# Two transformer blocks on one core: attention products in split passes, gates behind both halves, a shorter second norm

## The chip, the core and the metric

The kernel runs on one core of one Trainium2 chip. TensorE multiplies matrices, VectorE and ScalarE do elementwise work, GpSimd does a little of it and issues some transfers, and SP issues most transfers. The metric is the device time of one execution in microseconds (us).

## What is computed

The reference applies a first block (a gated mix of a convolution, a linear recurrence and stick-breaking attention, and a feed-forward part) and then a second block of two layers. The change touches the two layers, and one norm of the first block. A layer of the second block, with 512 positions, model width 1024 and 8 heads of width 128:

```python
x = x + 0.5 * swiglu(rms_norm_2(x, ffn1_norm[l]), ...)
h = rms_norm_2(x, mix_norm[l])
proj = h @ w_in[l] + b_in[l]
q, k, v, f_logit, xr, gr, g_attn, g_rnn = jnp.split(proj, SPLIT_POINTS, axis=-1)
q, k = rms_norm_2(q per head, q_norm[l]), rms_norm_2(k per head, k_norm[l])
log_f = jax.nn.log_sigmoid(f_logit)
y_attn = forgetting_attention(q, k, v, log_f) @ w_o_attn[l]
xr = causal_depthwise_conv(xr, conv_w[l], conv_b[l])
yr = rg_lru(xr, ...) * jax.nn.gelu(gr)
y_rnn = yr @ w_o_rnn[l]
merged = sigmoid(g_attn) * y_attn + sigmoid(g_rnn) * y_rnn
x = x + merged @ w_out[l]
x = x + 0.5 * swiglu(rms_norm_2(x, ffn2_norm[l]), ...)
```

`forgetting_attention` adds to the scaled scores of a causal softmax the difference of the running sums of `log_f` at the query and at the key. `rg_lru` is a gated linear recurrence over the positions.

## The kernel before

Activations lie transposed, as eight tiles of 128 channels by 512 positions, and every tile of 512 columns takes 2 KB of a partition.

**Split products.** A float32 matrix is kept as a high part rounded to float32r and the rest as a low part (`split`, line 221; `w`, line 182, does it for the weights). `mm3` (line 227) forms a product in three float32r passes: high by high, high by low, low by high. The projections are made in this way. Other products are plain float32 matmuls, which the profile lists as two records each: the scores (line 840), the values (line 865) and the recurrence's gates (lines 907 and 908). Transposes (lines 395 and 861) are matmuls against an identity, one record each.

**Weights** come in one order, written out in `_plan_layer`, through a ring of four chunks (`raw`, `hi`, `lo`): SP issues the load, ScalarE rounds (line 197), VectorE subtracts (line 198).

**Memory.** Tiles come from pools by tag, each tag with a number of buffers (`pool`, line 138). Pools are a stack: one that is opened after another was closed lies on the closed one's bytes. TensorE's results go to eight banks: four accumulators (`acc`, tag a), and four for everything else (xm, xh, two of xs). `tokens` (line 256) takes all four accumulators for a projection of queries, keys or values: for each weight chunk it runs the four token blocks in turn. `pair` (line 242) takes two.

**Order.** The framework orders each engine's instructions ahead of the run from a simulated timeline, by program order and with what stands under `hp()` first; a tile waits until a buffer of its tag is free.

**A mixing layer** (`mix`, line 959): the pool mb with 38 tiles (line 964). The recurrence's pool rn, 18 tiles and with them the tag xr, lives from line 983 to 1005: four pairs of projections, emptied by `scaled` (line 978) and line 1002 into xr, then `rnn` (line 892), which for each of eight tiles makes a convolution (lines 903 and 905), two products (907, 908), activations (910 to 914) and two multiplications (915, 916), and after every four tiles a square root (921), a product (923) and a scan (924). Then the forget gate: one accumulator `fa`, emptied into `fz` (line 1014), a scan, a transfer to memory (1021) from which `cb` is broadcast (884), and `ct` (1025). Then two halves of four heads each: queries, keys and values by `tokens`, emptied at line 1037, queries and keys normalised and transposed by `heads_T` into qkT (line 397), and `attn` (868). `attn_scores` (834) makes one block of 128 queries: product, bias (843), causal fill on GpSimd (845), maximum (848), exponential (849), scaling (851). `attn_values` (854) transposes the weights and multiplies them with the values, one block behind the scores; line 879 copies a finished head. After each half come the gates of the recurrence for that half (lines 1047 to 1059), written into tiles Y of a pool that is opened after the first half's attention (1045). Then the projections of the two branches with their gates, and the output projection.

**The second norm of the first block** (lines 578 to 594): line 583 adds the squares of each new tile to a running sum (`add_square`, line 305, whose addition is line 310); `stats` (296) then takes column products with ones (272), adds epsilon (280), takes the power on GpSimd (281), spreads the row by transposes (289) and copies it out (293), and lines 590 to 593 form the input of the feed-forward part.

Of the kernel before, what the change touches and what calls it, by code (L numbers as in the profile page):

```python
# [20 lines left out]
MIX = 3080  # L21
# [55 lines left out]
def _plan_layer(l):  # L77
# [4 lines left out]
    for hf in range(2):  # L82
        for o in (0, 1024, 2048):
            p += _rows("w_in_2", l, 8, o + hf * 512)
        for m in range(4 * hf, 4 * hf + 4, 2):
            p += _cols("w_in_2", l, 8, MIX + 1024 + m * 128)
# [32 lines left out]
class Build:  # L119
# [155 lines left out]

    def rsqrt(self, src, w, g="m"):
# [101 lines left out]
    def heads_T_(self, src, nh, dh, gain):  # L378
# [13 lines left out]
        for j in range(4):  # L392
# [3 lines left out]
            o = self.t("qkT")  # L396
            nc.scalar.activation(o, ps, AF.Copy, scale=gain)
            out.append(o)
# [164 lines left out]
    def first_block(self):  # L563
        nc = self.nc
        src = lambda i: self.ap["xT"][i * 128:i * 128 + 128, :]
        with ExitStack() as ctx:
# [5 lines left out]
            with ExitStack() as c1:  # L572
# [5 lines left out]
                for m in range(0, 8, 2):  # L578
                    for i, a in enumerate(self.pair("w_out", 0, 8, m * 128, mh)):
                        with self.hp():  # L580
                            nc.vector.scalar_tensor_tensor(x[m + i], a, self.mod[:, 16 + m + i:17 + m + i], x[m + i],
                                                           op0=OP.mult, op1=OP.add)
                            self.add_square(x[m + i], m + i == 0)
            self.pool(ctx, "mlp", act=32, t=4, mr=2)
            with self.hp():
                _, rb = self.stats()
# [247 lines left out]
    def attn_scores(self, qT, kT, i, hd, ct, cb):  # L834
# [5 lines left out]
        nc.tensor.matmul(ps[:, :n], qT[:, ts], kT[:, :n], start=True, stop=True)  # L840
# [13 lines left out]
    def attn_values(self, st, v, vc, i, o):  # L854

        nc = self.nc
        n = (i + 1) * 128
        pt = self.aux("xs")
        for j in range(i + 1):
            js = slice(j * 128, j * 128 + 128)  # L860
            nc.tensor.transpose(pt[:, js], st[:, js], self.ident)  # L861
        pT = self.t("pT")
        nc.scalar.copy(pT[:, :n], pt[:, :n])
        for j in range(i + 1):
            nc.tensor.matmul(o[:, i * 128:n], v[j][:, vc:vc + 128], pT[:, j * 128:j * 128 + 128],  # L865
                             start=(i == 0 and j == 0), stop=(i == 3 and j == 3), skip_group_check=True)

    def attn(self, qT, kT, v, hd0, ct, cdram):
# [3 lines left out]

        def values(st, hd, i):
            if i == 0:
                out.append(self.aux("xh"))
            self.attn_values(st, v, (hd - hd0) * 128, i, out[-1])
            if i == 3:
                y = self.t("x")
                nc.scalar.copy(y, out[-1])
                out[-1] = y  # L880

        for hd in range(hd0, hd0 + 4):
            cb = self.t("cb")
            nc.gpsimd.dma_start(cb, cdram[hd:hd + 1, :].to_broadcast([128, 512]))
            for i in range(4):
                todo.append((self.attn_scores(qT[hd - hd0], kT[hd - hd0], i, hd, ct, cb), hd, i))
                if len(todo) > 1:
                    values(*todo.pop(0))
        values(*todo.pop(0))
# [292 lines left out]
```

## Time and profile before

| | |
|---|---|
| median of 3 runs | 3414.53 us (3413.23 to 3414.99) |
| the profiled execution | 3413.82 us, its span 3412.0 us |
| TensorE busy | 3389.3 us, 15362 records |
| VectorE busy | 1879.7 us |
| ScalarE busy | 1308.1 us |
| GpSimd busy | 164.6 us |
| transfers | 351.30 MB, mean 103 GB/s |

The profile is one execution on the chip. Its page gives busy times of each engine, the span in 40 slices, and the chain of work that ended last; the trace answers for single lines, tiles and stretches. A matmul's record is longer than its slot, since matmuls overlap: the slot shows in the distance of starts, or in the chain, where each piece lasts until the next one begins.

### The profile page before, as it was taken

Reading aid. Unit: us, or ns where it says so; the run is one execution under the profiler, and the core shown is the slowest. Engines: PE = TensorE matmul, PEld = TensorE weight load, DVE = VectorE, ACT = ScalarE, POOL = GpSimd, SP = SyncE. Lnnn points to the kernel's source line nnn. Section 1 sums busy time; section 2 is a strip of 40 time slices with the busy share of each in tenths; the row PEclk is TensorE's granted clock in tenths of the full one; section 3 lists DMA queues with packets and bytes.
Section 4 is the critical chain, followed back from the end, with each engine's and each line's share of the span. In section 5 each row is a group of like instructions: output and inputs, shape, how many; then the busy total and the mean of one; then the engine's idle time right before and its main releaser. Section 6 shows DMA issues by size and latency. Waiting matters only on the chain.

```text
span 3412.0 us, 42001 instructions
## 1 busy us (share of the span) xinstructions
PE 3389.3 (99%) x15362; PEld 2767.3 (81%) x15362; DVE 1879.7 (55%) x3168; ACT 1308.1 (38%) x2283; POOL 164.6 (5%) x273
## 2 busy tenths in 40 slices
PE   8999999999999999999999999999999999999999
PEld 6887777888888888788888888888887788888887
DVE  7698654534444444876455444444447865454442
ACT  3335443423333333654333333333336544343331
POOL 0011000000000001111000000000010110000000
PEclk9999999999999999999999999999999999999999
DMA  6223433433333333323333333333333222333332
GB/s 217 72 78 106 154 112 107 130 98 97 96 96 97 96 117 105 90 91 89 111 97 95 99 97 97 95 99 96 103 123 95 86 89 81 123 95 98 96 105 91
DMA packets 179599, 351.30 MB, mean 103 GB/s; under 512 B 20672, under 2 KB 21952, under 8 KB 178368
## 3 DMA queue, kind: packets, MB, share of 16 engines
q1 hardware_dynamic: 173088, 329.05, 31.5%
q0 software_dynamic: 6160, 19.37, 1.9%
q8 instruction: 121, 1.98, 0.2%
q14 instruction: 86, 0.70, 0.1%
q10 hardware_dynamic: 144, 0.20, 0.0%
HBM read 342.21 MB, written 6.32 MB: 102 GB/s over the span
## 4 chain that ended last, share of the span: by engine, by line
PE 96%; DVE 2%; ACT 1%; issue 1%; DMA 0%; POOL 0%; SPq 0%; DVEq 0%; ACTq 0%
PE a L231 30%; PE a L229 30%; PE a L230 30%; PE xh L865 1%; PE xs L840 1%; PE xh L432 1%; PE xh L514 1%; PE xs L492 1%; PE xs L861 1%; PE xm L395 0%; DVE xc L905 0%; DVE mq L333 0%; DVE lo L198 0%; PE xh L508 0%; PE xh L471 0%
## 5 line engine op out<-in xcount | busy, mean ns | idle before, releaser
L198 DVE TENSOR_TENSOR lo<-raw,hi 128x512 fp32r<-128x512 f32 x1144 | 785.1, 688 | 1254.2 <-ACT hi L197 1239.7
L197 ACT CAST hi<-raw 128x512 fp32r<-128x512 f32 x1144 | 706.9, 619 | 1571.7 <-PE a L230 1270.4
L230 PE MATMUL a<-h,hi 128*128 128x512 f32 x2528 | 989.4, 392 | 0.0
L229 PE MATMUL a<-h,hi 128*128 128x512 f32 x2528 | 984.4, 392 | 2.3 <-ACT h L592 2.3
L231 PE MATMUL a<-h,lo 128*128 128x512 f32 x2528 | 982.3, 392 | 0.0
L229 PEld LDWEIGHTS a<-h,hi 128*128 128x128 f32 x2528 | 475.2, 188 | 106.4 <-issue 6.1
L231 PEld LDWEIGHTS a<-h,lo 128*128 128x128 f32 x2528 | 474.9, 188 | 105.2 <-issue 7.2
L230 PEld LDWEIGHTS a<-h,hi 128*128 128x128 f32 x2528 | 474.9, 188 | 101.4 <-issue 3.6
L229 PE MATMUL a<-act,hi 128*128 128x512 f32 x960 | 373.4, 389 | 0.0
L230 PE MATMUL a<-act,hi 128*128 128x512 f32 x960 | 373.4, 389 | 0.0
L231 PE MATMUL a<-act,lo 128*128 128x512 f32 x960 | 372.8, 389 | 0.0
L230 PE MATMUL a<-Y,hi 128*128 128x512 f32 x544 | 214.5, 394 | 0.0
L229 PE MATMUL a<-Y,hi 128*128 128x512 f32 x544 | 213.7, 393 | 0.0
L231 PE MATMUL a<-Y,lo 128*128 128x512 f32 x544 | 212.8, 391 | 0.0
L229 PEld LDWEIGHTS a<-act,hi 128*128 128x128 f32 x960 | 180.2, 188 | 37.5
L231 PEld LDWEIGHTS a<-act,lo 128*128 128x128 f32 x960 | 180.2, 188 | 37.5
L230 PEld LDWEIGHTS a<-act,hi 128*128 128x128 f32 x960 | 180.2, 188 | 37.3
L231 PE MATMUL a<-hi,h 128*128 128x512 f32 x512 | 204.5, 403 | 0.0
L230 PE MATMUL a<-lo,h 128*128 128x512 f32 x512 | 203.7, 398 | 0.0
L229 PE MATMUL a<-hi,h 128*128 128x512 f32 x512 | 199.2, 407 | 1.7 <-DVE qk L1037 1.7
L231 PEld LDWEIGHTS a<-Y,lo 128*128 128x128 f32 x544 | 102.2, 188 | 23.4 <-issue 2.1
L230 PEld LDWEIGHTS a<-Y,hi 128*128 128x128 f32 x544 | 102.2, 188 | 23.1 <-issue 2.0
(293 smaller groups left out, 3049.3 us busy)
## 6 DMA issues: line engine op xcount, KB each, us to landing
raw<-in_w_l SPq DMA_DIRECT2D x852, 256.0 KB, 2.6
raw<-in_w_first SPq DMA_DIRECT2D x284, 256.0 KB, 2.6
mr<-in_mod_b_ SPq DMA_DIRECT2D x32, 512.0 KB, 3.8
mq<-in_mod_a SPq DMA_DIRECT2D x8, 1024.0 KB, 8.1
xs<-x POOLq DMA_DIRECT2D x16, 256.0 KB, 2.4
cb<-cd POOLq DMA_DIRECT2D x16, 256.0 KB, 3.5
x<-xs POOLq DMA_DIRECT2D x16, 256.0 KB, 3.9
bq<-in_brow POOLq DMA_DIRECT2D x12, 256.0 KB, 3.8
```

The lines of the kernel that those rows point to most:

```text
L197: nc.scalar.copy(hi, raw)
L198: nc.vector.tensor_tensor(lo, raw, hi.bitcast(F32), op=OP.subtract)
L229: mm(acc, w[0], x[0], start=start, stop=False)
L230: mm(acc, w[0], x[1], start=False, stop=False)
L231: mm(acc, w[1], x[0], start=False, stop=stop)
L432: mm(ps[:, i * 64:i * 64 + 64], k[:, s], q[:, s].rearrange("p (n c h) -> p n c h", c=2, h=h)[:, :, 1], start=True, stop=True)
L492: mm(z[:, o:o + n], q[pr, blk(i)], k[pr, :n], start=True, stop=True)
L514: mm(pt[pr, c], v[j][:, hd * 64:hd * 64 + 64], f[:, o + j * 128:o + j * 128 + 128], start=j == 0, stop=j == i, skip_group_check=True)
L840: nc.tensor.matmul(ps[:, :n], qT[:, ts], kT[:, :n], start=True, stop=True)
L861: nc.tensor.transpose(pt[:, js], st[:, js], self.ident)
L865: nc.tensor.matmul(o[:, i * 128:n], v[j][:, vc:vc + 128], pT[:, j * 128:j * 128 + 128], start=(i == 0 and j == 0), stop=(i == 3 and j == 3 ...
```

## The change

- The scores and the values become split products. `heads_T` gets a flag with which queries and keys are split after the transpose; the values are split as they are emptied, through a tile of tag qk. `attn_values` now works on a whole head: for each block of 128 keys it transposes the weights of all query blocks that see it, takes a high part on ScalarE and a low part on VectorE, and runs three passes over 512, 384, 256 and 128 columns. `attn` makes the four score blocks of a head and calls the values of the head before after the second of them.
- The tiles of the attention move from the pool mb (now 17 tiles) to a pool at of 33 tiles, opened after the recurrence's pool is closed. The tag s has 5 buffers in place of 3, v 8 in place of 6, qkT 16 in place of 8.
- The gates of the recurrence come after both halves, write into the recurrence's own output tiles, and are split into Y after the pool at is closed and Y's pool opened. The order of the weights follows.
- The second norm takes the column products of the running sum over seven tiles and of the eighth square into one accumulation, and lines 590 to 593 read the spread row from TensorE's result bank.

```diff
--- before.py
+++ after.py
@@ -82,8 +82,8 @@
     for hf in range(2):
         for o in (0, 1024, 2048):
             p += _rows("w_in_2", l, 8, o + hf * 512)
-        for m in range(4 * hf, 4 * hf + 4, 2):
-            p += _cols("w_in_2", l, 8, MIX + 1024 + m * 128)
+    for m in range(0, 8, 2):
+        p += _cols("w_in_2", l, 8, MIX + 1024 + m * 128)
     for o, w in ((3072, "w_o_rnn_2"), (2048, "w_o_attn_2")):
         for m in range(0, 8, 2):
             p += _cols("w_in_2", l, 8, MIX + o + m * 128) + _cols(w, l, 8, m * 128)
@@ -273,6 +273,15 @@
                                   start=True, stop=True)
         return ps[:, 0:4]
 
+    def rows_of_sum(self, parts, scale, xt):
+
+        ps = self.aux(xt)
+        for n, p in enumerate(parts):
+            for i in range(4):
+                self.nc.tensor.matmul(ps[:, i:i + 1], p[:, i * 128:i * 128 + 128], self.ones[scale][:, 0:1],
+                                      start=n == i == 0, stop=n == len(parts) - 1, skip_group_check=True)
+        return ps[:, 0:4]
+
     def rsqrt(self, src, w, g="m"):
 
         nc = self.nc
@@ -375,7 +384,7 @@
         with self.hp():
             return self.heads_T_(*a)
 
-    def heads_T_(self, src, nh, dh, gain):
+    def heads_T_(self, src, nh, dh, gain, parts=False):
         nc = self.nc
         ms, m, r = [self.small(4 * nh) for _ in range(3)]
         for tt in range(4):
@@ -393,9 +402,9 @@
             ps = self.aux("xm" if "xm" in self.pxt else "xs")
             for tt in range(4):
                 nc.tensor.transpose(ps[:, tt * 128:tt * 128 + 128], src[tt][:, j * 128:j * 128 + 128], self.ident)
-            o = self.t("qkT")
+            o = self.t("t" if parts else "qkT")
             nc.scalar.activation(o, ps, AF.Copy, scale=gain)
-            out.append(o)
+            out.append(self.split(o, "qkT") if parts else o)
         return out
 
 
@@ -580,10 +589,12 @@
                         with self.hp():
                             nc.vector.scalar_tensor_tensor(x[m + i], a, self.mod[:, 16 + m + i:17 + m + i], x[m + i],
                                                            op0=OP.mult, op1=OP.add)
-                            self.add_square(x[m + i], m + i == 0)
+                            if m + i < 7:
+                                self.add_square(x[m + i], m + i == 0)
             self.pool(ctx, "mlp", act=32, t=4, mr=2)
             with self.hp():
-                _, rb = self.stats()
+                ps = self.rows_of_sum([self.p, self.square(x[7])], 1.0 / D, "xh")
+                rb = self.spread(self.rsqrt(ps, 4), "xh", out=False)
                 h2 = []
                 for i in range(8):
                     y, sh = self.t("t"), self.mod[:, 24 + i:25 + i]
@@ -837,7 +848,7 @@
         n = (i + 1) * 128
         ts = slice(i * 128, n)
         ps = self.aux("xs")
-        nc.tensor.matmul(ps[:, :n], qT[:, ts], kT[:, :n], start=True, stop=True)
+        self.mm3(ps[:, :n], [a[:, ts] for a in qT], [a[:, :n] for a in kT], True, True)
         st = self.t("s")
         s = st[:, :n]
         nc.vector.scalar_tensor_tensor(s, ps[:, :n], ct[:, i * 8 + hd:i * 8 + hd + 1], cb[:, :n],
@@ -851,42 +862,38 @@
         nc.vector.tensor_scalar(s, s, ri, None, op0=OP.mult)
         return st
 
-    def attn_values(self, st, v, vc, i, o):
-
-        nc = self.nc
-        n = (i + 1) * 128
-        pt = self.aux("xs")
-        for j in range(i + 1):
+    def attn_values(self, sts, v, vc):
+
+        nc = self.nc
+        o = self.aux("xh")
+        for j in range(4):
             js = slice(j * 128, j * 128 + 128)
-            nc.tensor.transpose(pt[:, js], st[:, js], self.ident)
-        pT = self.t("pT")
-        nc.scalar.copy(pT[:, :n], pt[:, :n])
-        for j in range(i + 1):
-            nc.tensor.matmul(o[:, i * 128:n], v[j][:, vc:vc + 128], pT[:, j * 128:j * 128 + 128],
-                             start=(i == 0 and j == 0), stop=(i == 3 and j == 3), skip_group_check=True)
+            n = 512 - j * 128
+            pt = self.aux("xs")
+            for i in range(j, 4):
+                nc.tensor.transpose(pt[:, (i - j) * 128:(i - j) * 128 + 128], sts[i][:, js], self.ident)
+            hi, lo = self.t("pT", F32R), self.t("pT", F32R)
+            nc.scalar.copy(hi[:, :n], pt[:, :n])
+            nc.vector.tensor_tensor(lo[:, :n], pt[:, :n], hi[:, :n].bitcast(F32), op=OP.subtract)
+            self.mm3(o[:, j * 128:], [a[:, vc:vc + 128] for a in v[j]], (hi[:, :n], lo[:, :n]), j == 0, j == 3)
+        y = self.t("x")
+        nc.scalar.copy(y, o)
+        return y
 
     def attn(self, qT, kT, v, hd0, ct, cdram):
 
         nc = self.nc
         out, todo = [], []
-
-        def values(st, hd, i):
-            if i == 0:
-                out.append(self.aux("xh"))
-            self.attn_values(st, v, (hd - hd0) * 128, i, out[-1])
-            if i == 3:
-                y = self.t("x")
-                nc.scalar.copy(y, out[-1])
-                out[-1] = y
-
         for hd in range(hd0, hd0 + 4):
             cb = self.t("cb")
             nc.gpsimd.dma_start(cb, cdram[hd:hd + 1, :].to_broadcast([128, 512]))
+            sts = []
             for i in range(4):
-                todo.append((self.attn_scores(qT[hd - hd0], kT[hd - hd0], i, hd, ct, cb), hd, i))
-                if len(todo) > 1:
-                    values(*todo.pop(0))
-        values(*todo.pop(0))
+                sts.append(self.attn_scores(qT[hd - hd0], kT[hd - hd0], i, hd, ct, cb))
+                if i == 1 and todo:
+                    out.append(self.attn_values(*todo.pop(0)))
+            todo.append((sts, v, (hd - hd0) * 128))
+        out.append(self.attn_values(*todo.pop(0)))
         return out
 
     def rnn(self, xr, bd, l, hb, sp4):
@@ -961,7 +968,7 @@
         h = self.hx
         with ExitStack() as ctx:
             lp = ctx.enter_context(self.tc.tile_pool(name=f"lp{l}", bufs=1))
-            self.pool(ctx, f"mb{l}", hm=8, t=3, bq=1, qk=5, v=6, qkT=8, cb=2, s=3, pT=2)
+            self.pool(ctx, f"mb{l}", hm=8, t=3, bq=1, qk=5)
             with self.hp():
                 rt, rb = self.stats()
             hb = self.lined(lp, (128, 32), name="hb")
@@ -1003,6 +1010,8 @@
                         xr.append(u)
                 hs = self.rnn(xr, bd, l, hb, sp4)
                 self.tap(f"hs{l}", hs[0])
+            c3 = ctx.enter_context(ExitStack())
+            self.pool(c3, f"at{l}", cb=2, s=5, pT=2, v=8, qkT=16)
 
             fa = self.acc()
             for k0 in (0, 4):
@@ -1032,31 +1041,31 @@
                     nc.gpsimd.dma_start(bq, self.ap["brow"][l:l + 1, c:c + 512].to_broadcast([128, 512]))
                     ts = []
                     for tt, a in enumerate(self.tokens("w_in_2", l, c, h)):
-                        v = self.t("v" if n == 2 else "qk")
+                        v = self.t("qk")
                         with self.hp():
                             nc.vector.scalar_tensor_tensor(v, a, rt[:, tt:tt + 1], bq, op0=OP.mult, op1=OP.add)
-                        ts.append(v)
+                            ts.append(self.split(v, "v") if n == 2 else v)
                     if n == 0:
-                        qT = self.heads_T(ts, 4, 128, qg)
+                        qT = self.heads_T(ts, 4, 128, qg, True)
                     elif n == 1:
-                        kT = self.heads_T(ts, 4, 128, self.col(("k_norm_2", l)))
+                        kT = self.heads_T(ts, 4, 128, self.col(("k_norm_2", l)), True)
                 ya += self.attn(qT, kT, ts, hf * 4, ct, cdram)
-                if hf == 0:
-                    self.pool(ctx, f"my{l}", Y=16)
-                    yr = []
-                for m in range(4 * hf, 4 * hf + 4, 2):
-                    for i, a in enumerate(self.pair("w_in_2", l, 8, MIX + 1024 + m * 128, h)):
...
-                            nc.vector.scalar_tensor_tensor(z, z, 0.5, hs[m + i], op0=OP.mult, op1=OP.mult)
-                            yr.append(self.split(z, "Y"))
+            for m in range(0, 8, 2):
+                for i, a in enumerate(self.pair("w_in_2", l, 8, MIX + 1024 + m * 128, h)):
+                    with self.hp():
+                        z, w = scaled(a, "t"), self.t("sq")
+                        bz = self.col(("b_mix", l), 8 + m + i)
...
+                        nc.vector.scalar_tensor_tensor(hs[m + i], z, 0.5, hs[m + i], op0=OP.mult, op1=OP.mult)
+            c3.close()
+            self.pool(ctx, f"my{l}", Y=16)
+            with self.hp():
+                yr = [self.split(y, "Y") for y in hs]
             self.tap(f"yr{l}", yr[0][0].bitcast(F32))
             mg = [None] * 8
             for n, (o, wn) in enumerate(((3072, "w_o_rnn_2"), (2048, "w_o_attn_2"))):
```

## Rows read from the trace of the kernel before

**Rows 1.** The page: busy us, share of the span and records of each engine.
```profile
PE 3389.3 (99%) x15362; PEld 2767.3 (81%) x15362; DVE 1879.7 (55%) x3168; ACT 1308.1 (38%) x2283; POOL 164.6 (5%) x273
```

**Rows 2.** Windows: us, busy us (x records) by engine, granted clock, DMA share, GB/s.
```profile
1340.00:1460.00 120.00, 118.77 (x511) 91.82 (x510) 92.53 (x152) 77.77 (x123) 11.99 (x14) 1.00 0.29 89
1700.00:1800.00 100.00, 100.00 (x443) 82.81 (x442) 52.65 (x82) 35.91 (x59) 0.00 (x0) 1.00 0.32 97
587.40:597.40 10.00, 6.20 (x19) 4.82 (x20) 5.04 (x9) 3.24 (x5) 1.03 (x1) 0.50 0.23 90
```

**Rows 3.** Chain in time: start us, us to the next piece, what (x records).
```profile
1370.06 0.91 PE a L229 x4
...
1553.36 0.66 PE xs L840 x4
...
1602.24 0.44 PE xs L861 x4
...
1607.69 0.89 PE xh L865 x8
...
1608.69 0.65 PE xs L840 x2
...
1614.11 0.86 PE xs L840 x2
```

**Rows 4.** Timeline of the second norm: start us, us, engine, line, [idle before, releaser].
```profile
586.72 0.68 DVE L310 TENSOR_TENSOR p<-p,sq 128x512 f32<-128x512 f32 x1
...
587.55 1.84 PE L272 MATMUL xh<-oned,p 128*128 128x1 f32 x8 [2.74 <-DVE p L310]
...
591.91 0.59 ACT L293 COPY rb<-xh 128x512 f32<-128x512 f32 x1 [5.58 <-PE xh L289]
...
594.15 0.80 PE L229 MATMUL a<-h,hi 128*128 128x512 f32 x1 [2.28 <-ACT h L592]
```

**Rows 5.** Groups, 1340 to 1660 us: line, operation, count, busy us, mean ns.
```profile
L198 DVE TENSOR_TENSOR lo<-raw,hi 128x512 fp32r<-128x512 f32 x93 | 63.1, 685 | 44.7 <-ACT hi L197 44.6
...
L223 ACT CAST Y<-t 128x512 fp32r<-128x512 f32 x8 | 5.0, 620 | 2.6 <-DVE t L1058 2.6
```

**Rows 6.** Timeline where the two mixing layers open: GpSimd, and TensorE's last act.
```profile
1304.32 0.39 PE L231 MATMUL a<-act,lo 128*128 128x512 f32 x1
...
1304.37 0.54 POOL L803 DMA_DIRECT2D xs<-x  x1 [28.02 <-DVE x L828]
1304.90 1.95 POOL L989 MEMSET bd<- 128x512 f32 x4
...
2536.81 1.95 POOL L989 MEMSET bd<- 128x512 f32 x4
```

**Rows 7.** Timeline of VectorE: last projection emptied, fz, last scan, first layer.
```profile
1348.32 0.69 DVE L978 TENSOR_TENSOR t<-a,rb 128x512 f32<-128x512 f32 x1 [0.24 <-PE a L231]
...
1357.77 0.67 DVE L1014 TENSOR_TENSOR s<-a,rb 8x512 f32<-8x512 f32 x1
...
1450.54 1.21 DVE L924 TENSOR_TENSOR_SCAN hm<-hm,abc 128x512 f32<-128x512 f32 x1
```

**Rows 8.** Timeline of the recurrence: activation of tiles 1 and 8, a convolution, chain.
```profile
1350.54 0.69 ACT L910 ACTIVATE abc<-xs,hb 128x512 f32<-128x512 f32 x1 [0.47 <-PE xs L907]
...
1403.62 0.54 DVE L903 TENSOR_SCALAR xc<-xr,cv 128x512 f32<-128x512 f32 x1
...
1407.21 0.74 DVE L905 SCALAR_TENSOR_TENSOR xc<-xr,cv,xc 128x512 f32<-128x512 f32 x1
...
1422.16 0.86 PE xs L907 x2
...
1437.31 0.69 ACT L910 ACTIVATE abc<-xs,hb 128x512 f32<-128x512 f32 x1 [0.86 <-PE xs L907]
```

**Rows 9.** Timeline of ScalarE: copies of the second half's first and last head.
```profile
1584.87 0.59 ACT L879 COPY x<-xh 128x512 f32<-128x512 f32 x1
...
1652.98 0.58 ACT L879 COPY x<-xh 128x512 f32<-128x512 f32 x1
```

More of the change, by code (lines that the diff above doesn't have):

```diff
@@ L1041, in mix @@
                     elif n == 1:
-                        kT = self.heads_T(ts, 4, 128, self.col(("k_norm_2", l)))
+                        kT = self.heads_T(ts, 4, 128, self.col(("k_norm_2", l)), True)
                 ya += self.attn(qT, kT, ts, hf * 4, ct, cdram)
-                if hf == 0:
-                    self.pool(ctx, f"my{l}", Y=16)
-                    yr = []
-                for m in range(4 * hf, 4 * hf + 4, 2):
-                    for i, a in enumerate(self.pair("w_in_2", l, 8, MIX + 1024 + m * 128, h)):
-                        with self.hp():
-                            z, w = scaled(a, "t"), self.t("sq")
-                            bz = self.col(("b_mix", l), 8 + m + i)
-                            nc.vector.tensor_scalar(z, z, bz, None, op0=OP.add)
-                            nc.scalar.activation(w, z, AF.Square)
-                            nc.vector.tensor_scalar(w, w, 0.044715, 1.0, op0=OP.mult, op1=OP.add)
-                            nc.vector.tensor_tensor(w, w, z, op=OP.mult)
-                            nc.scalar.activation(w, w, AF.Tanh, scale=0.7978845608028654)
-                            nc.vector.scalar_tensor_tensor(z, w, 1.0, z, op0=OP.add, op1=OP.mult)
-                            nc.vector.scalar_tensor_tensor(z, z, 0.5, hs[m + i], op0=OP.mult, op1=OP.mult)
-                            yr.append(self.split(z, "Y"))
@@ new lines, in mix @@
+            for m in range(0, 8, 2):
[3 more added lines that the diff above has]
+                        bz = self.col(("b_mix", l), 8 + m + i)
+                        nc.vector.tensor_scalar(z, z, bz, None, op0=OP.add)
+                        nc.scalar.activation(w, z, AF.Square)
+                        nc.vector.tensor_scalar(w, w, 0.044715, 1.0, op0=OP.mult, op1=OP.add)
+                        nc.vector.tensor_tensor(w, w, z, op=OP.mult)
+                        nc.scalar.activation(w, w, AF.Tanh, scale=0.7978845608028654)
+                        nc.vector.scalar_tensor_tensor(z, w, 1.0, z, op0=OP.add, op1=OP.mult)
+                        nc.vector.scalar_tensor_tensor(hs[m + i], z, 0.5, hs[m + i], op0=OP.mult, op1=OP.mult)
```

## The prediction

> **What bounds the kernel now.** I read the page first: TensorE is busy 99% of the span, VectorE 55% and ScalarE 38% [rows 1]. A busy TensorE could still be a slow one, so next I read the windows: a plain stretch of projections, 1700 to 1800 us, holds 443 records in 100 us [rows 2], and the chain lists four such passes in 0.91 us [rows 3], so a 512-wide pass of the split product costs 0.227 us and nothing is lost between passes. The mixing stretch from 1340 to 1460 us shows 118.8 of 120 us busy at the full clock, while VectorE works 92.5 us and ScalarE 77.8 us of it [rows 2]. So the end is set by the sum of TensorE's slots, and an edit is worth what it takes off that sum, as long as it opens no hole in it. Two questions follow: what the new passes cost, and whether something that TensorE waits for becomes late.
>
> **The attention products.** Priced from the chain of work, which lists TensorE's slots back to back [rows 3]. One head before: the four score products are two records each, 0.86 us at width 512, 0.65 at 384 and 0.66 for 128 and 256 together, 2.17 us in all; the ten value products of width 128 are 20 records, of which eight take 0.89 us, so 2.22 us. After: three passes each over widths 512, 384, 256 and 128, once for scores and once for values. The trace has no such pass narrower than 512. At 512 it costs 0.227 us, about half of one plain record (0.43). Half of the plain records at 384 and 256 is 0.163 and 0.109; a 128-wide single-pass transpose takes 0.11 (four in 0.44), and I let nothing be cheaper. That gives 0.61 for the four widths, 1.83 for three passes, 3.66 us for both products, against 4.39: 0.73 us a head less, 11.7 us over 16 heads. The bound on the other side is that narrow passes cost a full plain record (0.325, 0.219, 0.111): 2.65 us a product, 14.4 us more over 16 heads. I take the saving, because the 512 row is nearest, and keep both ends.
>
> The Trainium skill ("TensorE: Matmul & The Clock Gate", section "Back-to-back issue gap") gives a warm pass as its width over 2.4 GHz plus 2.5 ns. By that, an estimate, the four widths take 0.54 us and 16 heads save 18 us; the trace has 0.227 where the rule gives 0.216, so the sum keeps the trace's prices.
>
> **The second norm.** It happens once. TensorE stands from the last output projection to 594.15 us. The change takes the last addition (0.68) and the copy of the spread row (0.59) out of this chain [rows 4], and adds four column products; the four there take 1.84 us as eight records [rows 4], of which the half that reads the running sum can go first. Between 0.4 and 1.3 us less; I take 1.
>
> **Splits and copies.** Each layer gains 24 splits of 512 columns (16 for queries and keys, 8 for values) and 32 low parts of the weights: on VectorE at most 56 x 0.68, 38 us, and on ScalarE 24 x 0.62, 15 us [rows 5]. Beside TensorE's work these cost nothing; VectorE's idle time in the stretch covers them. If that cover goes they reappear in the attention's own latency, priced below.
>
> **The pool that is opened where the recurrence closed.** This is the step that decides. Before, the tiles of the attention (s, v, qkT, cb, pT) lie in the layer's first pool, 38 tiles of 2 KB, beside the recurrence's pool. After, they are 33 tiles in a pool of their own, opened on the spot where the recurrence's pool was just closed. The tile framework holds every tile of such a pool until all users of the closed one are done. The trace shows the same at the start of a layer: the clearing of bd needs no input, and GpSimd had idled for 28 us until a transfer at 1304.37, yet it was put behind that transfer and starts at 1304.90, after the last matmul that reads act (tiles of the pool closed before) began at 1304.32 [rows 6].
>
> Now follow the first tile of the new pool. It is fz (line 1014), which empties the accumulator of the forget gate. Before, this ran at 1357.8, while the last scan of the recurrence ran at 1450.5 to 1451.8 [rows 7]: 93 us later. After, line 1014 has to stand behind that scan. The forget gate then keeps one of four accumulators, and the query projection needs all four: its fourth token block cannot start, the four weight chunks in the ring are not released, and TensorE runs dry. The copies of cb on the GpSimd queue wait for the same pool, but are needed later.
>
> What TensorE can still do from the last recurrence projection (emptied at 1348.3 [rows 7]): the forget gate, 24 passes, 5.4 us; three token blocks over four chunks, 36 passes, 8.2 us; the recurrence's own 16 products at 0.86 us [rows 8], 13.8 us. Together 27.4 us, so its work ends at an equivalent of 1375.7 us. What lies between that and the end of the recurrence is lost.
>
> When does the recurrence end after the change? At the old pace at 1451.8, plus 0.67 for line 1014: 76.7 us lost. But the old pace was set by company: from the first gate activation at 1350.5 to the eighth at 1437.3 [rows 8] is 12.4 us a tile, in which VectorE also emptied and normalised queries and keys and TensorE queued the products behind projections. With these gone a round is the convolution, 4.3 us from 1403.6 to 1407.95 with the two multiplications in between [rows 8], a product, and the first activation after it, some 5.5 us; with waits in the fixed order of VectorE up to 9, and the idle TensorE falls to the half clock, as it did for 10 us around the second norm (0.50 [rows 2]), which doubles the 0.86. I take 8 us a round: the eighth activation at 1406.5, and the same tail of 14.5 us (1437.3 to 1451.8) to 1421, or 48 us lost after rounding up for the clock's share (1424). Ends: 27 us (5.5 a round) and 77 us. The restart at half clock costs some 2 us (after the second norm it restarted at 594.15, at 0.50 until 597.4, [rows 2, 4]). Two layers: 100 us.
>
> **The gates moved behind both halves.** Their 192 passes (43.6 us) stay the same work, and SP's queue loads the same chunks: eight of the sixteen move behind the second half's 24, in the order of use. But the pool of Y is now opened where the attention's pool closes, so the recurrent projection waits for the last head. From the first half's last key to there TensorE has the values (21.8), the second half's three projections (65.4 and 3.5 of transposes), the gates (43.6), the first gate pair of the output (10.9) and eight heads at 4.8: 183 us, 22.9 us a head. Before, the last three heads took 68.1 us, 22.7 a head [rows 9]. Even, so I charge 3 us a layer; VectorE's 38 us more could make it 25, and a shorter chain nothing.
>
> **Sum.** The profiled execution took 3413.8 us (span 3412.0 and 1.8 around it); the median is 3414.5, 0.7 above. 3413.8 - 11.7 - 1 + 100 + 6 = 3507 us.
>
> **Rivals.** *The recurrence keeps its pace.* Its rounds could be bound by their own fixed order rather than by company. For it: VectorE still idles 27 of the 120 us in that stretch. Against it: 4.3 us for a convolution that shares the engine. 3401 + 2 x (76.7 + 2) + 6 gives 3564 us, and with the late Y at 25 a layer 3608.
> *Not slower: the wait is hidden or absent.* If tiles waited one by one, s could land on bytes that the recurrence frees early, and line 1014 would run near 1358 as before. It would have to be freed by about 1376, the point where TensorE's other work ends. Then only the slots count: 3413.8 - 11.7 - 1 = 3401 us, and with narrow passes at the 128-wide plain price of 0.222 for a whole product, 10.8 us dearer, 3412. Against it: GpSimd waits in the same way in the second layer, with the clearing at 2536.81 [rows 6]. The Trainium skill ("SBUF — State Buffer", section "Specifications (TRN2)") gives about 208 KiB usable in a partition; by my count of tiles, an estimate, the two pools side by side would bring the layer to 232 KiB, so they cannot but share. No run here shows that figure.
> *The wait is there and short.* A round of 5.5 us and a tail that overlaps give 27 us a layer: 3401 + 54 + 4, 3459 us.
>
> **How the numbers follow.** Forecast 0.60 (3465 to 3550 by itself), recurrence at its old pace 0.16, short wait 0.13, no wait 0.11. The range 3440 to 3585 leaves out the no-wait case, half of the slow one. About 0.2% can be told from no change here: the no-wait case splits into faster 0.08 and same 0.03; slower 0.89.
>
> **What would show it.** In the profile after: line 1014 right behind the last scan of each layer; before it a stretch of tens of us where TensorE runs only lines 907 and 908 and the granted clock drops to half; activations of line 910 closer together than 12 us; the split passes of the attention at 0.11 to 0.23 us in the chain; the first Y soon after the last copy of line 879. If line 1014 runs while scans are still to come, the main step is wrong. If the attention's passes take a full plain record, the saving is wrong. If TensorE waits for Y at the recurrent projection, the gates' move costs more than I charge.

## The result, and the profile after

The changed kernel takes 3574.4 us (3573.8 to 3575.6), the kernel before 3414.7 on the same chip: a ratio of 1.0468, 95% interval 1.0455 to 1.0481, 160 us slower. The forecast was 3507, 93 us slower. The profiled execution took 3574.7 us, its span is 3572.9.

The page of the changed kernel, beside [rows 1]: TensorE's busy time, the slices of the span for TensorE and its granted clock, and one group of instructions.

```profile
PE 3450.1 (97%) x15306; PEld 2791.6 (78%) x15306; DVE 1941.0 (54%) x3279; ACT 1339.2 (37%) x2330; POOL 154.9 (4%) x273
...
PE   8999999999999995998999999999995998999999
...
PEclk9999999999999997997999999999997998999999
...
L229 PE MATMUL a<-hi,h 128*128 128x512 f32 x512 | 193.5, 403 | 25.7 <-DVE s L1023 23.2
```

Each layer now has two dips; the prediction foresaw the first, and charged little for the second. The last row names the first: token projections waited 23.2 us in the two layers together for line 1023, which empties the forget gate into fz (line 1014 before). Busy time rose although there are fewer records, since records are longer at the half clock (rows of line 914 below).

Windows of the changed kernel (columns as in [rows 2]): the two dips of layer 1, those of layer 2, and a plain stretch.

```profile
1360.00:1430.00 70.00, 31.61 (x65) 14.65 (x64) 40.13 (x58) 39.91 (x57) 0.55 (x3) 0.66 0.00 1
1630.00:1700.00 70.00, 56.62 (x198) 40.17 (x197) 41.05 (x99) 29.29 (x71) 6.62 (x18) 0.71 0.08 26
1700.00:1800.00 100.00, 100.00 (x443) 82.81 (x442) 44.30 (x67) 33.92 (x55) 4.39 (x8) 1.00 0.39 119
2670.00:2745.00 75.00, 37.52 (x86) 19.05 (x85) 44.29 (x65) 41.60 (x60) 0.90 (x4) 0.68 0.03 9
2945.00:3010.00 65.00, 51.09 (x181) 34.72 (x181) 39.51 (x96) 28.21 (x70) 6.50 (x18) 0.74 0.07 23
```

Idle time alone understates a dip, since what runs in it runs at the half clock. So a stretch's *lost time* here is its length less what its passes take at the full clock (0.227 us for a 512-wide pass, 0.11 to 0.175 for narrower ones, 0.43 for a plain 512-wide record). Layer 1 loses 50.1 us from 1340 to 1430 (hole A), 2.6 from there to 1630, and 37.4 from 1630 to 1700 (hole B); layer 2 loses 50.1 (2655 to 2745) and 35.6 (2945 to 3012). The kernel before lost 3.2 us from 1340 to 1700.

**Hole A.** Timeline of TensorE and VectorE in layer 1 (columns as in [rows 6]):

```profile
1367.09 1.10 PE L914 MATMUL xs<-xc,bd 128*128 128x512 f32 x2 [0.75 <-DVE xc L912]
...
1373.92 2.04 PE L914 MATMUL xs<-xc,bd 128*128 128x512 f32 x2 [4.87 <-DVE xc L912]
...
1408.54 2.05 PE L914 MATMUL xs<-xc,bd 128*128 128x512 f32 x2 [4.03 <-DVE xc L912]
...
1420.71 2.33 DVE L931 TENSOR_TENSOR_SCAN hm<-hm,abc 128x512 f32<-128x512 f32 x2
1423.13 0.68 DVE L1023 TENSOR_TENSOR s<-a,rb 8x512 f32<-8x512 f32 x1
1423.87 0.80 PE L229 MATMUL a<-hi,h 128*128 128x512 f32 x1 [11.58 <-DVE s L1023]
```

This is the step that the prediction called decisive. Line 1023 stands right behind the last scan (in [rows 7] it ran 93 us ahead of it), and until then TensorE has only the recurrence's products (lines 914 and 915), each pair of which soon waits 4 to 7 us, mostly for a convolution (line 912).

**Hole B.** Timeline of ScalarE, the rows of two lines alone: line 876 rounds a block of transposed weights into the high part pT, line 880 copies a finished head (here the third head, then the sixth, then the copy of the eighth).

```profile
1574.00 0.58 ACT L876 CAST pT<-xs 128x512 fp32r<-128x512 f32 x1
...
1577.88 0.47 ACT L876 CAST pT<-xs 128x384 fp32r<-128x384 f32 x1
...
1585.03 0.37 ACT L876 CAST pT<-xs 128x256 fp32r<-128x256 f32 x1 [0.69 <-PE xh L230]
...
1591.00 0.27 ACT L876 CAST pT<-xs 128x128 fp32r<-128x128 f32 x1 [0.19 <-PE xh L230]
...
1597.20 0.57 ACT L880 COPY x<-xh 128x512 f32<-128x512 f32 x1
...
1654.21 0.59 ACT L876 CAST pT<-xs 128x512 fp32r<-128x512 f32 x1
...
1656.46 0.48 ACT L876 CAST pT<-xs 128x384 fp32r<-128x384 f32 x1 [0.98 <-PE xh L230]
1658.31 0.37 ACT L876 CAST pT<-xs 128x256 fp32r<-128x256 f32 x1 [1.37 <-PE xh L230]
1659.81 0.27 ACT L876 CAST pT<-xs 128x128 fp32r<-128x128 f32 x1 [1.13 <-PE xh L230]
1661.52 0.59 ACT L880 COPY x<-xh 128x512 f32<-128x512 f32 x1 [1.44 <-PE xh L231]
...
1686.91 0.58 ACT L880 COPY x<-xh 128x512 f32<-128x512 f32 x1
```

A head's values are four steps, one for each block of 128 keys: transpose, round, subtract, three passes. There is one pair of pT tiles, so a rounding waits for passes of the step before (line 230, the second of the three). Alone, a step takes 1.5 to 2.3 us (1654.2, 1656.5, 1658.3, 1659.8). In company it takes 4 to 7 (1574.0 to 1591.0): TensorE's order is fixed ahead of the run, and 18 to 20 passes of a projection lie ahead of the passes of the second, third and fourth step. The copies of the first four heads come at 1532, 1564, 1597 and 1634 us, some 34 us apart, those of the last four 13 us apart. In the kernel before they were 22.7 us apart at the end [rows 9]. The last gate of the recurrence was projected by 1620 us and the first gate pair of the output by 1633, so four heads were left with nothing beside them. The output projection waits for Y, and Y's pool for the last head: the timeline of TensorE has its first pass right behind.

```profile
584.50 0.39 PE L231 MATMUL a<-Y,lo 128*128 128x512 f32 x1
...
593.52 2.07 PE L229 MATMUL a<-h,hi 128*128 128x512 f32 x4 [1.65 <-ACT h L603]
...
1687.05 1.22 PE L229 MATMUL a<-Y,hi 128*128 128x512 f32 x2 [0.71 <-ACT Y L223]
```

The second of these rows is the restart after the second norm. It stands 9.02 us behind the last pass before the norm, the first row; in the kernel before these were 9.73 us (584.42 to 594.15 [rows 4]), so the norm is 0.71 us shorter. The row of the kernel before:

```profile
584.42 0.39 PE L231 MATMUL a<-Y,lo 128*128 128x512 f32 x1
```

**The passes.** The chain of the changed kernel in layer 2 (columns as in [rows 3]) has scores of 384 and 512 columns, then a pass of 128 and one of 256.

```profile
2807.48 0.17 PE xs L229
2807.65 0.18 PE xs L230
2807.83 0.18 PE xs L231
2808.00 0.24 PE xs L229
...
2812.65 0.11 PE xs L230
...
2814.64 0.12 PE xs L230
```

A head's two products cost 6 x (0.235 + 0.175 + 0.12 + 0.11) = 3.84 us, by the forecast 3.66, before 4.39.

### The profile page after: what moved, and what is told of

It is laid out like the page before. It is cut to its first block, busy times and chain, and to the rows that moved or that the text cites. A ratio compares the mean times of both kernels' runs of the same rounds, so it can differ in the third digit from the quotient of the medians.

```text
span 3572.9 us, 42096 instructions
## 1 busy us (share of the span) xinstructions
PE 3450.1 (97%) x15306; PEld 2791.6 (78%) x15306; DVE 1941.0 (54%) x3279; ACT 1339.2 (37%) x2330; POOL 154.9 (4%) x273
## 5 line engine op out<-in xcount | busy, mean ns | idle before, releaser
L229 PE MATMUL a<-hi,h 128*128 128x512 f32 x512 | 193.5, 403 | 25.7 <-DVE s L1023 23.2
L230 PEld LDWEIGHTS a<-act,hi 128*128 128x128 f32 x960 | 180.2, 188 | 37.4
L229 PEld LDWEIGHTS a<-act,hi 128*128 128x128 f32 x960 | 180.2, 188 | 37.4
L231 PE MATMUL a<-hi,h 128*128 128x512 f32 x512 | 202.4, 396 | 0.0
L229 PEld LDWEIGHTS a<-hi,h 128*128 128x128 f32 x512 | 96.3, 190 | 50.1 <-DVE s L1023 26.3
```

Source lines behind the costliest of these rows:

```text
L229: mm(acc, w[0], x[0], start=start, stop=False)
L230: mm(acc, w[0], x[1], start=False, stop=False)
L231: mm(acc, w[1], x[0], start=False, stop=stop)
```

## The experiments

The theory: the 160 us are holes A and B (50 and 37 us a layer), less some 10 us that the split passes save. All ratios are against the kernel before, which took 3414.6 to 3415.2 us beside these runs; gains are differences of medians.

**Hole A alone.** In the kernel before, the attention's tiles leave the first pool:

```diff
-            self.pool(ctx, f"mb{l}", hm=8, t=3, bq=1, qk=5, v=6, qkT=8, cb=2, s=3, pT=2)
+            self.pool(ctx, f"mb{l}", hm=8, t=3, bq=1, qk=5)
...
                 self.tap(f"hs{l}", hs[0])
+            self.pool(ctx, f"at{l}", cb=2, s=3, pT=2, v=6, qkT=8)
```

> The kernel before, with one thing changed: the attention's tiles (cb, s, pT, v, qkT, old buffer counts) leave the layer's first pool for one opened where the recurrence's pool has closed. Products, gates and the second norm stay. The theory is that the changed kernel loses its time at two places in each layer: some 50 us ahead of the emptying of the forget gate (the hole A), and some 37 us in the second half's heads (the hole B). Of these only A should be here: 3414.5 + 2 x 50, about 3515 us, and TensorE with nothing but the recurrence's products for tens of us in each layer. The rival, that A comes from the extra splits and copies on VectorE and not from the pool, expects 3415 to 3425 us.

Measured: 3511.4 us, ratio 1.0283 (1.0268 to 1.0299), 96.5 us slower. Its windows over the places of A and B:

```profile
1360.00:1430.00 70.00, 32.45 (x63) 15.40 (x63) 39.80 (x57) 39.52 (x57) 0.55 (x3) 0.66 0.01 3
1640.00:1700.00 60.00, 60.00 (x299) 49.56 (x298) 31.77 (x64) 24.07 (x52) 3.15 (x10) 1.00 0.26 79
```

The first row is that of the changed kernel almost to the record; the second has no hole. So A is the pool's place and nothing else of the change, and B is not a consequence of A. Nor does the pool slow the heads: with the old chain, the last four copies stand 23.7, 23.3 and 21.3 us apart in this run, and 23.7, 23.3 and 21.1 in the kernel before.

**fz out of the late pool.** In the changed kernel:

```diff
-            fz, fe, fc = [self.t("s")[0:8] for _ in range(3)]
+            fz, fe, fc = [self.t("qk")[0:8] for _ in range(3)]
```

> The changed kernel, with fz, fe and fc taken from the tag qk of the layer's first pool in place of s of the late pool. If A is one accumulator held by the forget gate, fz runs before the recurrence's end, and TensorE gains the rest of the query projection (13.6 us) and up to the whole key projection (21.8 us) as work beside the recurrence; queries and keys still need tiles of the late pool to get further. So 14 to 35 us less in each layer, 3505 to 3547 us. The rival, that the transposed queries and keys (also of the late pool) are what holds TensorE, and fz is only the first to show it, expects about 3560 to 3575 us.

Measured: 3510.7 us, ratio 1.0281 (1.0265 to 1.0296): 31.8 us less in each layer, near the upper end. The windows over A and the (now earlier) last heads:

```profile
1360.00:1430.00 70.00, 69.17 (x291) 52.34 (x291) 54.43 (x87) 46.06 (x71) 5.01 (x7) 1.00 0.27 80
1600.00:1660.00 60.00, 47.87 (x152) 32.24 (x153) 35.59 (x90) 25.49 (x64) 5.99 (x18) 0.64 0.04 9
```

One accumulator that could not be emptied held nearly two thirds of A. The rest comes a little later (13.2 us lost from 1430 to 1500); that queries and keys, which need the late pool too, are what holds it there is argued from the order of the program, and tried with the early tiles below. B stays.

**The gates back between the halves.**

```diff
-            for m in range(0, 8, 2):
-                for i, a in enumerate(self.pair("w_in_2", l, 8, MIX + 1024 + m * 128, h)):
+                for m in range(4 * hf, 4 * hf + 4, 2):
+                    for i, a in enumerate(self.pair("w_in_2", l, 8, MIX + 1024 + m * 128, h)):
```

> The changed kernel, with the recurrence's gates put back as two groups of four, one after each half of the heads; they still write into the recurrence's own tiles, and Y still comes after the last head. If B is the second half's heads left without other work for TensorE, the second group (21.8 us of passes a layer) fills so much of the 37 us: 3574 - 2 x 22 = about 3530 us. If B is the wait for Y's pool alone, with heads as slow as they are in any case, the end moves by less than 5 us a layer: 3565 to 3575 us. The hole A stays at 50 us in both.

Measured: 3579.6 us, ratio 1.0482 (1.0466 to 1.0498), 5 us more than the changed kernel and outside both ranges. The timeline has the last gate on VectorE and the copies of heads four and five:

```profile
1627.74 0.69 DVE L1063 SCALAR_TENSOR_TENSOR t<-sq,t 128x512 f32<-128x512 f32 x1
...
1637.00 0.57 ACT L880 COPY x<-xh 128x512 f32<-128x512 f32 x1
...
1650.87 0.59 ACT L880 COPY x<-xh 128x512 f32<-128x512 f32 x1 [1.24 <-PE xh L231]
```

The theory in this form falls. The second group does stand behind the second half's heads in the program, but it was used up at 1628, while the fourth head was still under way. Where the gates stand is not what makes B; that the heads are behind schedule is.

**Deeper buffers, and pT alone** (the second run leaves s at 5).

```diff
-            self.pool(c3, f"at{l}", cb=2, s=5, pT=2, v=8, qkT=16)
+            self.pool(c3, f"at{l}", cb=2, s=8, pT=4, v=8, qkT=16)
```

> The changed kernel, with 8 buffers of s in place of 5 and 4 of pT in place of 2 (10 KB of a partition more). If B is long because a head is a chain of steps that each wait for the one buffer pair of pT (12.9 us a head), a head falls to some 8 to 10 us and B from 37 to about 20 us a layer: 3530 to 3550 us. If the buffers are not what a head waits for, 3570 to 3575 us.

> The changed kernel with 4 buffers of pT in place of 2, s left at 5. Of the 39.5 us that deeper buffers of both gave: if the one pair of pT makes the chain (the next rounding of a transposed block waits until the passes over the block before it have run), nearly all of it is here, 3535 to 3545 us. If it is s (the next head's score blocks wait for the values of the head before), 3565 to 3575 us.

Measured: 3534.9 us (1.0351, 1.0334 to 1.0369) with both, 39.5 less; 3547.5 us (1.0387, 1.0373 to 1.0401) with pT alone, 26.9 less. With both, the first and the fourth head end at

```profile
1518.80 0.58 ACT L880 COPY x<-xh 128x512 f32<-128x512 f32 x1
...
1591.31 0.59 ACT L880 COPY x<-xh 128x512 f32<-128x512 f32 x1
```

24 us a head in place of 34, and B loses 16 us in layer 1 in place of 37, with A unchanged. With pT alone it is some 28 us a head, and B loses 22. So B hangs on the heads' pace in company. pT gives two thirds of the gain; s gives the rest, against the expectation that pT would give nearly all (3535 to 3545 us, missed by 2.5).

**Early tiles back in the first pool**, without and with the gates in two groups:

```diff
-        st = self.t("s")
+        st = self.t("s" if i < 2 else "s2")
...
-            self.pool(ctx, f"mb{l}", hm=8, t=3, bq=1, qk=5)
+            self.pool(ctx, f"mb{l}", hm=8, t=3, bq=1, qk=5, cb=2, s=3, qkT=16)
...
-            self.pool(c3, f"at{l}", cb=2, s=5, pT=2, v=8, qkT=16)
+            self.pool(c3, f"at{l}", s2=5, pT=4, v=8)
```

> The changed kernel, with its tiles shared out by when they are needed: cb, three buffers of s (for the first two score blocks of a head and for fz, fe, fc) and all sixteen of qkT go back into the layer's first pool; only what is needed after the recurrence (five buffers for the last two score blocks of a head, four of pT, eight of v) stays in the late pool. If A is the wait of tiles that are needed early, it goes (100 us), and the deeper buffers take some 40 us of B, as in the run before: 3574 - 140 = about 3435 us. If the recurrence and the attention's first half now get in each other's way on VectorE, so that TensorE runs dry later instead, 3450 to 3480 us.

> The same, and the recurrence's gates in two groups, one after each half of the heads. If what is left of B (some 16 us a layer in the run with deeper buffers) is want of other work in the second half, and the first half's heads now end before the second group is used up, it goes: 3403 to 3412 us, faster than the kernel before by the attention's 12 us less what is left of the holes. If the groups are used up ahead of the heads as in the run with gates put back, no better than the kernel without them, within 6 us.

Measured: 3465.9 us (1.0148, 1.0134 to 1.0162) and 3466.6 us (1.0150, 1.0136 to 1.0164). The windows of the first over A's place and over its last heads:

```profile
1400.00:1455.00 55.00, 48.86 (x209) 36.74 (x208) 46.39 (x75) 37.95 (x61) 5.08 (x5) 0.94 0.25 73
1598.00:1635.00 37.00, 26.16 (x102) 18.90 (x103) 20.52 (x54) 14.00 (x37) 3.50 (x11) 0.77 0.06 15
```

108.5 us come back, not 140: A falls from 50 to some 10 us a layer, and B stays at some 23. The rival's range (3450 to 3480) held, but its cause isn't shown: VectorE, now with recurrence and queries at once, works 46 of 55 us there, yet in the run with three pairs below it works 49.8 and only 3.9 are lost. The gates in two groups again change nothing.

**Work ahead of Y.** Output gate pairs, which need no Y, are projected first, into qk: two pairs on the kernel with the early tiles (gates behind both halves), three (with s, s2 and qk shared out as its expectation tells), and two on the changed kernel itself.

```diff
+PAIRS = ([(1, 0), (1, 2), (0, 0), (0, 2), (1, 4), (0, 4), (1, 6), (0, 6)],
+         [(g, m) for m in range(0, 8, 2) for g in (1, 0)])
...
-                for m in range(0, 8, 2):
-                    ga = self.pair("w_in_2", l, 8, MIX + o + m * 128, h)
+                ga = {}
+                for gate, m in PAIRS[n]:
+                    if gate:
+                        acc = self.pair("w_in_2", l, 8, MIX + o + m * 128, h)
...
```

> The changed kernel with the early tiles in the first pool, as two runs before (3465.9 us there; some 23 us a layer of idle TensorE left in the last four heads, some 10 us around the recurrence's end), and one thing more: the first two pairs of the recurrent branch's output gates are projected ahead of the first output projection, into the tag qk, which nothing else needs by then. Those passes need no Y. If B is TensorE left with nothing that it may run until Y's pool opens behind the last head, the second pair's 10.9 us fill that much of it in each layer: 3466 - 22 = about 3444 us. If B is the price of the heads whatever stands beside them, 3460 to 3468 us.

> The same with three pairs ahead (qk has six buffers, s two, for the first score block of a head and no longer for fz, fe and fc, which take qk; the other three score blocks have six buffers in the late pool, so that a head does not wait for the tiles of the one before). By the theory 21.8 us of B are filled in each layer, which is nearly all of it, and the score blocks come earlier: 3415 to 3430 us. If the first head, now with three of its four score blocks behind the recurrence's end, is what TensorE waits for, 3435 to 3450 us.

> The changed kernel itself, and only the two pairs of output gates ahead of the first output projection. B alone is touched: with 10.9 us more in each layer that TensorE may run before Y, 3574 - 22 = about 3552 us. If the heads only become slower by what is put between them, as with the gates in two groups, 3570 to 3580 us.

Measured: 3456.3 us (1.0123, 1.0109 to 1.0137), 3440.6 us (1.0077, 1.0064 to 1.0089) and 3566.6 us (1.0447, 1.0431 to 1.0463). Two pairs give 9.6 and 7.8 us where 22 were expected. Other work does count, but at less than half its length: TensorE takes it up while the fifth head is under way, and the last three heads run alone as before, 12 us each. Three pairs with the other buffers give 25 us, of which some 12 are in A (4 us lost a layer in place of 10) and the rest in B:

```profile
1400.00:1455.00 55.00, 52.40 (x238) 40.71 (x237) 49.80 (x82) 40.37 (x68) 5.74 (x6) 1.00 0.26 77
```

The forecast of 3415 to 3430 was missed. The time lies in the other range, 3435 to 3450, but not for its reason, since the loss around the first head became smaller. Two things changed at once here (pairs and buffers), so what each gave is not shown.

**Y off the attention's bytes.** The high part of Y goes into the recurrence's own tiles, the low part into eight tiles beside v; s and qkT go back into the first pool, as the expectation tells:

```diff
-            self.pool(c3, f"at{l}", cb=2, s=5, pT=2, v=8, qkT=16)
+            self.pool(c3, f"at{l}", pT=2, v=8, Yl=8)
...
-                        nc.vector.scalar_tensor_tensor(hs[m + i], z, 0.5, hs[m + i], op0=OP.mult, op1=OP.mult)
-            c3.close()
-            self.pool(ctx, f"my{l}", Y=16)
-            with self.hp():
-                yr = [self.split(y, "Y") for y in hs]
+                        nc.vector.scalar_tensor_tensor(z, z, 0.5, hs[m + i], op0=OP.mult, op1=OP.mult)
+                        hi, lo = self.t("hm", F32R), self.t("Yl", F32R)
+                        nc.scalar.copy(hi, z)
+                        nc.vector.tensor_tensor(lo, z, hi.bitcast(F32), op=OP.subtract)
+                        yr.append((hi, lo))
```

> The changed kernel with all that the early steps need in the first pool (s and qkT; cb goes through two single tiles that lie idle here), buffers as in the changed kernel (five of s, one pair of pT), and with Y no longer on the attention's bytes: the high parts take the recurrence's own tiles, the low parts eight tiles beside v, and each is split as soon as its gate is there. So the recurrent output projection (87 us a layer) may run beside the second half's heads, as in the kernel before. The gates stay behind both halves. If Y's place is what makes B, then B goes although the heads have no deeper buffers; what is left is some 10 us a layer around the recurrence's end: 3401 + 20, so 3415 to 3430 us. If the heads' own chain makes B wherever Y lies, some 15 to 35 us a layer stay at the last heads: 3445 to 3490 us.

Measured: 3456.3 us (1.0123, 1.0106 to 1.0139). The last heads' window:

```profile
1655.00:1685.00 30.00, 22.63 (x79) 15.84 (x78) 18.45 (x41) 11.97 (x28) 6.67 (x13) 0.72 0.25 79
```

With pT and s as shallow as in the changed kernel, B loses 17.6 us in place of 37.4, and comes later: the recurrent output projection now runs beside the heads, but at 33 to 44 us a head that work too is used up before the last of them. So neither the place of Y nor the heads' chain makes all of B by itself: it is what is left of eight slow heads when the other work is out. The rival's range (3445 to 3490) held, though B halved. A head with deep buffers and a Y without the pool were not tried together.

**The second norm alone**, in the kernel before.

```diff
-                            self.add_square(x[m + i], m + i == 0)
+                            if m + i < 7:
+                                self.add_square(x[m + i], m + i == 0)
...
-                _, rb = self.stats()
+                ps = self.rows_of_sum([self.p, self.square(x[7])], 1.0 / D, "xh")
+                rb = self.spread(self.rsqrt(ps, 4), "xh", out=False)
```

> The kernel before with the second norm of the changed kernel and nothing else. By the sum of the prediction 0.4 to 1.3 us less than before, 3413.6 to 3414.5 us beside 3414.9. If the chain through VectorE was not what TensorE waited for there, no difference.

Measured: 3414.5 us beside 3415.2, ratio 0.9997 (0.9988 to 1.0006). By times it can't be told from nothing; by the trace of the changed kernel the norm is 0.71 us shorter.

## Why the prediction was right, and where it was short

The direction was right, and 3574 lies in the range of 3440 to 3585, near its upper end. That it does is in part luck: the forecast's own band was 3465 to 3550, with at most 25 us a layer for the late Y, and the range reached further only for a slow recurrence, which did not come. The steps one by one:

- *The late pool: right, in mechanism and size.* Forecast 100 us for two layers, found 2 x 50.1 of lost time in the changed kernel, and 96.5 us by its own experiment. The round of 8 us was 8.3 (products from 1367.1 to 1408.5, five rounds), fz was expected behind 1421 us and ran at 1423.1. fz and one accumulator were indeed the larger part, two thirds. Of the 15 us a layer that stay without them (2.0 up to 1430 us and the 13.2 behind it), 5 go when the tiles of scores, queries and keys move too, which the step did not name; what holds the other 10 is open.
- *The gates and Y's pool: the failed term.* The prediction charged 3 us a layer (0 to 25) and the changed kernel loses 36.5 on average: 73 us in place of 6, nearly all of the miss of 67. The step that failed is the sentence that spread 183 us of work over eight heads, 22.9 us a head, and called it even with the 22.7 of [rows 9]. Those 22.7 belonged to another chain: before, the values of one block followed one block behind its scores. The new head has four value steps in a row through one pair of pT and s for one block ahead; in company that is 34 us. The first four heads took the work that was meant for eight, and the other four ran alone: (13.1 - 4.9) x 4 = 33 us, with 4.9 us of TensorE's own work a head (3.84 + ten transposes of 0.11). The prediction had priced the attention's slots and never its new chain. That the chain is at fault is shown by the runs with deeper buffers (34, 28 and 24 us a head go with 37, 22 and 16 us of B) and by the old chain's pace in the first experiment; beyond pT and s, which of its links costs what was not tested, nor were the moved gates with the old chain. The prediction did name the sign to look for, TensorE waiting for Y at the recurrent projection.
- *The attention products: right, priced a little too low.* Forecast 11.7 us; by the chain 16 x (4.39 - 3.84) = 8.8. Set against the time: 177.7 us lost in the stretches 1340 to 1700 and 2655 to 3012, less 2 x 3.2 before, less 0.7 for the norm, leave 170.6, and 159.7 were measured, so 11. Between 9 and 11 us.
- *The second norm: right* in the trace (0.71 in a range of 0.4 to 1.3), too small for the times.
- *Splits and copies: at nothing was right while TensorE had work:* between the holes the changed kernel loses 2.6 us a layer. In hole B a rounding and a subtraction are links of each step of the chain. Whether they have a part in the 10 us that stay of A where recurrence and queries run side by side was not tested.
- *The rivals.* The time is near the 3564 of "the recurrence keeps its pace", but that is not what happened: the recurrence ended at 1423 us, not at 1452. Without the trace the right time would have confirmed the wrong story. In the rival without a wait, the 10.8 us for narrow passes follow only if each 128-wide pass costs 0.222 us, not a whole product; it cost 0.11.

No version found here beats the kernel before. The best, with early tiles in the first pool and three gate pairs ahead, is at 3440.6 us: it keeps the saving and still loses some 20 us a layer to the last heads and the recurrence's end.

## What to carry to other kernels

When an edit changes how many dependent steps a chain has, or how many buffers it runs through, don't take its old pace for the new one: count its hand-overs, price each by what the engine that they share runs ahead of it, and ask how many links are left when the other work is out. A pool opened on the bytes of a closed one holds back whatever is emptied first into it; put there only what is needed after the closed one's last user. Other work moved next to a slow chain may be used up before the chain gets there, so moving it buys less than its length.

## What the runs showed of the hardware that was not expected

A float32r pass over 128 columns, with a weight load of its own as every pass here, costs nearly as much as one over 256: 0.11 and 0.12 us, where 512 take 0.235 and 384 take 0.175. The Trainium skill ("TensorE: Matmul & The Clock Gate", section "Back-to-back issue gap") puts the sustained spacing of such pairs of load and pass at about 81 ns for 128 columns and 131 for 512, without naming a type, and gives the formula that the prediction cites for an isolated matmul; this trace disagrees with both spacings, 110 and 235 ns, and its own decide here.

In hole A the granted clock was 0.51 from 1372 to 1386 us, the lower of the two levels (1.2 GHz in place of 2.4), while TensorE ran only a pair of products every 7 to 10 us: the two records of line 914 took 1.10 us at 1367.09 and 2.04 at 1373.92. In hole B it was 0.65 on average from 1640 to 1686 us, while TensorE was at no time idle for more than 1.72 us there.
